# Eight transposes of an attention unit written as one run, and a planner that counts changes of product kind

## The chip, the cores and the metric

The kernel runs on one core of a Trainium2 chip. A core has TensorE (matrix products and transposes, results into PSUM banks), VectorE, ScalarE and GpSimd for everything elementwise, and SyncE (SP), which issues DMAs. In the profile these are PE, DVE, ACT, POOL and SP; PEld is TensorE's loading of the stationary operand. The metric is the device time of one execution in microseconds.

## The reference

Two layers of an encoder trunk on 512 tokens of width 1024, in float32. Cut to what matters:

```
for l in range(DEPTH):                          # DEPTH = 2
    x = x + hybrid_mixer(rms_norm(x), ...)      # 8 heads of neighbourhood attention (NA) beside
                                                # 8 query heads of grouped-query attention (GQA)
    x = x + memory_cross_attention(rms_norm(x), rms_norm(mem), ...)
    x = x + conv_ffn(rms_norm(x), ...)
return rms_norm(x, norm_final)

# both attentions: scores = q k^T (+ bias), p = softmax(scores), o = p v
```

The softmaxed scores p come out with queries on the partitions. For `p v` they are needed with keys on the partitions, so every unit of p is transposed on TensorE.

## The kernel before

Activations lie transposed, channels on partitions and the 512 tokens along the row. A float32 operand is split into a high and a low part of the type fp32r, and a product of two such operands is three matmuls (`mm3`: hi x hi, hi x lo, lo x hi). These are one kind of product. The other kind takes full float32 operands: the transposes (data against `ident`), the sums over partitions (against `ones`) and the rows that spread a norm over the partitions.

Attention is done in units. An NA unit is a pair of heads and two blocks of 128 queries (8 units a layer), a GQA unit a pair of query heads and one block of 128 queries (16 units a layer). Each goes through four steps: scores on TensorE (`na_scores`, `gqa_scores`, into `sc` banks), exponent on ScalarE, division by the sum (`na_normalise`, `gqa_normalise`), transposes (`na_transpose`, `gqa_transpose_p`), values (`na_values`, and `gqa_values` after every fourth unit). `weave` interleaves the steps of successive units, and `Filler` puts the projections, w_out and memory products between them.

A unit has two halves, one per head, each a tile `t` of 128 x 512 scores: four transposes of 128 x 128 into one PSUM bank `tr`, then a cast to the high part on ScalarE and a subtraction for the low part on VectorE (`split_psum`), which frees the bank. There are two `tr` banks. Before, each half asked for its bank, wrote its four transposes and was split, one half after the other. The GQA queries and keys (`gqa_q`, `gqa_k`) are turned in the same manner, four transposes into one bank at a time, through `transposed`.

The order in which TensorE, ScalarE, VectorE and GpSimd do their work is not the written one. `Order`, called at the end, takes every traced instruction, gives it a duration by a table (`Step.times`; a transpose 108 ns, a product of n columns (n + 32) / 2.4 ns), and simulates the engines, the buffers (`SLOTS`) and the DMAs. For TensorE `product_next` looks through up to 240 products not yet issued, in the written order, and takes the first that can start within `PATIENCE` = 60 ns of the engine being free; for the others `choose` goes by due times. It repeats this for 30 rounds with changed due times, replays each with jitter, and keeps the order with the earliest simulated end. SP's queue stays in the written order.

Of the kernel before, what the change touches and what calls it, by code (L numbers as in the profile page):

```python
# [19 lines left out]
P = 128  # L20
# [186 lines left out]
HAND_OVER = {"PE": 60.0, "ACT": 85.0, "DVE": 60.0, "POOL": 80.0, "SP": 60.0}  # L207
STATIONARY = 100.0
FIRST_PRODUCT = 5000.0

# [13 lines left out]
class Step:  # L224
# [5 lines left out]
    def __init__(self, ins, index):  # L230
        self.ins, self.index, self.engine = ins, index, self.ENGINES[ins.engine]
        self.dma = type(ins).__name__ == "InstDMACopy"
        self.reads, self.writes = ([p for p in map(self.part, v) if p] for v in (ins.ins, ins.outs))
        self.names = list(dict.fromkeys(p[0] for p in self.writes + self.reads))
        self.bytes = 4.0 * self.count(ins.outs[0].bass_ap.ap) if self.dma else 0.0
        if self.dma and self.reads:

            self.bytes *= 1.5 if self.writes else 0.4
        self.busy, self.takes = self.times()
        self.sharing = self.shares()  # L240

# [88 lines left out]
class Order:  # L330
# [6 lines left out]

    def __init__(self, tc, kept):
        self.tc = tc
        traced = [i for i in tc.nc.cur_bb.bb.instructions if type(i).__name__ != "BassTilePoolBoundary"]  # L340
# [3 lines left out]
        for s in self.steps:  # L344
            if s.ins.name in kept and s.engine in last:
                self.kept[s.index] = last[s.engine]
            last[s.engine] = s.index
        self.lifetimes()

# [27 lines left out]
    def data(self):  # L377
# [4 lines left out]
        for s in self.steps:  # L382
# [17 lines left out]
            for j in self.before[-1]:  # L400
                self.after[j].append(s.index)

    def wait(self, a, b):
# [49 lines left out]
    def run(self, given=None, draw=None):  # L453
# [16 lines left out]

        moving, clock, last = [], 0.0, 0.0

        def possible(j, ready):

            if need[j] or self.kept.get(j, -1) >= 0 and self.kept[j] not in issued:
                return None
            if j in self.gate and self.gate[j] not in landed:
                return None
            t, wanted = ready[j], {}
            for name in steps[j].names:  # L480
                k = steps[j].kind(name)
                if name not in held and k in slots:

# [109 lines left out]
        while len(issued) < n or moving:  # L593
# [31 lines left out]
            if e == "PE":  # L625
                short = MARGIN - (t - possible(j, fed))
                if product is not None and short > 0:
                    late.append((j, t - product, t - product + short))
                product = t + s.busy
# [26 lines left out]
def encoder_kernel(ctx: ExitStack, tc: tile.TileContext, t: dict, out: bass.AP):  # L656
    nc = tc.nc
    kept = set()
    PE, SP = Counted(nc.tensor), InOrder(tc, nc.sync, kept)
# [496 lines left out]
    for l in range(DEPTH):  # L1156
# [181 lines left out]


        na = {}  # L1340
        parts = [None] * 8
# [40 lines left out]
        def na_transpose(u):  # L1382
            es = na[u]
            pts = []
            for j in range(2):
                tr = ps_t()
                for i in range(2):
                    for c in range(2):
                        PE.transpose(tr[:, (2 * i + c) * P : (2 * i + c + 1) * P], es[j][:, i, c * P : (c + 1) * P], ident)  # L1389
                pt = rtile((2, S))  # L1390
# [64 lines left out]

        def transposed(cc):
            tr = ps_t()
            for c in range(4):
                PE.transpose(tr[:, c * P : (c + 1) * P], cc[:, c * P : (c + 1) * P], ident)  # L1459
            return tr  # L1460

        def gqa_k(xs, cc, sq):
# [11 lines left out]
            def turn():  # L1474
                gk.extend(rtile((2, S)) for _ in range(2))
                split_k(transposed(cc), gk, False)

# [7 lines left out]
        def gqa_q(b, pm):  # L1485
# [11 lines left out]
            def turn():  # L1497
                gq[b] = rtile((2, S))
                split_q(transposed(cc), gq[b])

# [32 lines left out]
        def gqa_transpose_p(u):  # L1533
            es = ga.pop(u)
            i, b = divmod(u, NB)
            if b == 0:
                gpt[i] = []
                for j in range(2):
                    w = xpool.tile([P, KC, S], F32R, tag="xg", name=nm("xg"), bufs=2)
                    gpt[i].append(w.rearrange("p (n k) (b q) -> p n k b q", n=2, q=P))  # L1540
            for j in range(2):
                tr = ps_t()
                for k in range(NB):
                    PE.transpose(tr[:, k * P : (k + 1) * P], es[j][:, k * P : (k + 1) * P], ident)  # L1544
                hi, lo = (gpt[i][j][:, n, :, b] for n in range(2))
# [467 lines left out]

    Order(tc, kept)

# [82 lines left out]
```

## Time and profile before

| | us |
|---|---|
| median of 3 runs | 1315.31 (1315.18 to 1323.04) |
| profiled execution | 1314.66 |
| its span, first to last instruction | 1312.9 |
| TensorE busy in the span | 1302.0 |
| NA units' transposes (L1389), first and last start | 58.7 and 780.0 |
| GQA units' transposes (L1544), first and last start | 144.8 and 865.9 |
| granted TensorE clock | 1.00 |

All times in the traces count from the start of the span. A row of the timeline has the start, the length, the engine, the line, the operation, the tile written and the tiles read, the shape and a count; in brackets stands idle time of the engine before it and what ended it. Matmuls are pipelined: a row's length runs past the start of the next row, so the pace of TensorE is read from start to start. A transpose shows as one matmul of 128 columns.

### The profile page before, as it was taken

How to read it: one execution, taken by the hardware profiler on the slowest of the kernel's cores; microseconds unless marked ns; L12 is line 12 of the kernel's file. 1: busy time of each engine (PE TensorE's matmuls, PEld its weight loads, DVE VectorE, ACT ScalarE, POOL GpSimd, SP SyncE). 2: the span in 40 equal slices, each digit the busy share in tenths (PEclk: the TensorE clock that was granted, in tenths of full speed). 3: DMA queues.
4: the chain of work that ended last, by engine and by line, in shares of the span. 5: the costliest groups of instructions: out<-in, count | busy, mean ns of one | idle time of the engine just before them, and what ended most of it. 6: DMA issues, size and time to landing. Idle time of an engine off the chain costs nothing.

```text
span 1312.9 us, 21053 instructions
## 1 busy us (share of the span) xinstructions
PE 1302.0 (99%) x7632; PEld 1146.1 (87%) x7632; DVE 996.2 (76%) x1858; ACT 786.5 (60%) x1458; POOL 719.9 (55%) x520
## 2 busy tenths in 40 slices
PE   9999999999999999999999999999999999999998
PEld 8888888888789999999888888888887999999987
DVE  6559877675999887788535688776759999877874
ACT  6668876555655555545536688775645555555544
POOL 2757955726454454445746569565454544444443
PEclk9999999999999999999999999999999999999999
DMA  8733322313223333333455523223222333333332
GB/s 255 214 112 112 113 64 66 111 34 113 81 64 105 114 104 100 97 95 103 136 150 169 153 75 108 59 77 91 65 81 85 89 89 105 111 98 89 109 103 76
DMA packets 205000, 136.98 MB, mean 104 GB/s; under 512 B 5600, under 2 KB 195040, under 8 KB 204896
## 3 DMA queue, kind: packets, MB, share of 16 engines
q1 hardware_dynamic: 204080, 134.98, 35.3%
q8 instruction: 60, 0.98, 0.3%
q10 hardware_dynamic: 816, 0.66, 0.2%
q14 instruction: 44, 0.36, 0.1%
HBM read 125.65 MB, written 2.10 MB: 97 GB/s over the span
## 4 chain that ended last, share of the span: by engine, by line
PE 93%; DVE 4%; ACT 2%; issue 1%; DMA 0%; POOLq 0%; POOL 0%; SPq 0%; ACTq 0%; DVEq 0%
PE mm L103 63%; PE sc L103 21%; PE tr L103 4%; PE tr L1544 2%; DVE t L1837 1%; PE tr L1389 1%; PE tr L1731 1%; DVE r L1857 1%; DVE r L1038 0%; ACT hi L742 0%; PE tr L1459 0%; ACT t L1367 0%; DMA xT<-in_xT 0%; DVE xg L1866 0%; DVE t L1447 0%
## 5 line engine op out<-in xcount | busy, mean ns | idle before, releaser
L743 POOL TENSOR_TENSOR lo<-raw,hi 128x512 fp32r<-128x512 f32 (+3 forms) x230 | 369.4, 1620 | 281.0 <-ACT hi L742 233.5
L103 PE MATMUL mm<-r,hi 128*128 128x512 f32 (+1 forms) x1392 | 395.7, 365 | 0.0
L103 PEld LDWEIGHTS mm<-r,hi 128*128 128x128 f32 x1392 | 245.3, 189 | 34.9
L103 PE MATMUL mm<-xg,hi 128*128 128x512 f32 (+1 forms) x960 | 267.7, 364 | 1.5 <-DVE xg L1866 0.6
L103 PE MATMUL mm<-r,lo 128*128 128x512 f32 (+1 forms) x728 | 258.0, 356 | 0.0
L742 ACT CAST hi<-raw 128x512 fp32r<-128x512 f32 (+3 forms) x234 | 167.7, 738 | 134.1 <-PE mm L103 49.9
L103 PEld LDWEIGHTS mm<-xg,hi 128*128 128x128 f32 x960 | 169.9, 189 | 30.8 <-DVE xg L1866 3.3
L103 PE MATMUL mm<-xg,lo 128*128 128x512 f32 (+1 forms) x480 | 173.4, 361 | 0.0
L103 PE MATMUL sc<-r,hi 128*128 128x256 f32 (+1 forms) x832 | 162.9, 291 | 0.0
L754 POOL TENSOR_TENSOR lo<-sf,hi 128x1024 fp32r<-128x1024 f32 x32 | 78.0, 2437 | 148.0 <-ACT hi L751 101.0
L103 PEld LDWEIGHTS mm<-r,lo 128*128 128x128 f32 x728 | 137.5, 189 | 20.0
L103 PEld LDWEIGHTS sc<-r,hi 128*128 128x128 f32 x832 | 133.7, 191 | 4.9
L103 PE MATMUL sc<-r,lo 128*128 128x256 f32 (+1 forms) x416 | 121.2, 291 | 0.0
L751 ACT CAST hi<-sf 128x1024 fp32r<-128x1024 f32 x64 | 67.1, 1048 | 87.6 <-DVE sf L766 38.7
L103 PE MATMUL mm<-hi,xg 128*128 128x512 f32 (+1 forms) x384 | 111.4, 360 | 0.3 <-DVE r L1238 0.3
L103 PEld LDWEIGHTS mm<-xg,lo 128*128 128x128 f32 x480 | 90.7, 189 | 13.9
L754 POOL TENSOR_TENSOR lo<-raw,hi 128x1024 fp32r<-128x1024 f32 x32 | 78.0, 2436 | 43.6 <-ACT hi L751 36.9
L1044 POOL TENSOR_SCALAR t<-t,s 128x512 f32<-128x512 f32 (+1 forms) x112 | 66.8, 611 | 50.0 <-DVE s L1528 27.3
L103 PEld LDWEIGHTS sc<-r,lo 128*128 128x128 f32 x416 | 79.6, 191 | 1.2
L103 PEld LDWEIGHTS mm<-hi,xg 128*128 128x128 f32 x384 | 68.1, 190 | 9.4 <-DVE r L1238 0.6
L103 PE MATMUL sc<-r,r 128*128 128x256 f32 (+1 forms) x352 | 73.9, 330 | 0.0
L103 PE MATMUL mm<-lo,xg 128*128 128x512 f32 (+1 forms) x192 | 68.4, 356 | 0.0
(202 smaller groups left out, 2608.8 us busy)
## 6 DMA issues: line engine op xcount, KB each, us to landing
raw<-in_w_up SPq DMA_DIRECT2D x88, 512.0 KB, 3.8
raw<-in_w_down SPq DMA_DIRECT2D x36, 384.0 KB, 3.5
raw<-in_w_in SPq DMA_DIRECT2D x25, 512.0 KB, 4.8
raw<-in_w_mem_kv SPq DMA_DIRECT2D x16, 512.0 KB, 4.2
raw<-in_w_down SPq DMA_DIRECT2D x24, 320.0 KB, 3.2
r<-in_bias SPq DMA_DIRECT2D x16, 384.0 KB, 5.1
r<-r SPq DMA_DIRECT2D x22, 256.0 KB, 3.5
raw<-in_w_in SPq DMA_DIRECT2D x18, 256.0 KB, 4.7
```

The lines of the kernel that those rows point to most:

```text
L103: return self.engine.matmul(out, lhsT, rhs, **k)
L742: act.copy(hi[:, k], raw[:, k])
L743: (POOL if eng[0] == "P" else DVE).tensor_sub(lo[:, k], raw[:, k], f(hi)[:, k])
L751: act.copy(hi, src)
L754: eng.tensor_sub(lo[:, c], src[:, c], f(hi)[:, c])
L1044: eng.tensor_scalar(e, e, sums[:, col : col + 1], 1.0, op0=ALU.mult, op1=ALU.mult)
L1389: PE.transpose(tr[:, (2 * i + c) * P : (2 * i + c + 1) * P], es[j][:, i, c * P : (c + 1) * P], ident)
L1544: PE.transpose(tr[:, k * P : (k + 1) * P], es[j][:, k * P : (k + 1) * P], ident)
L1731: PE.transpose(tr[:, (2 * c + i) * P : (2 * c + i + 1) * P], e[:, i, c * P : (c + 1) * P], ident)
L1837: DVE.scalar_tensor_tensor(cc[:, dst], u[:, src], wi, cc[:, dst], op0=ALU.mult, op1=ALU.add)
L1857: DVE.scalar_tensor_tensor(xn[c // 2][:, c % 2], xT[c], ffn.gain(c), ffn.psum, op0=ALU.mult, op1=ALU.mult)
```

## The change

A new function `turned` asks for as many `tr` banks as it is given blocks, and writes the four transposes of every block directly after each other. `na_transpose` and `gqa_transpose_p` give it both halves of a unit, so eight transposes; the two splits follow. The queries and keys go through it with one block. The names of the transposes of each call are handed to `Order` as a group.

`Order.together` makes the first transpose of a group wait for everything that any of the group waits for, and has it ask for all the group's banks at once. The planner gets a constant `SWITCH` of 88 ns, which it adds to TensorE's time whenever a product without full float32 operands follows one with them. And after a full-float32 product, `product_next` first looks for another one that can start within 60 ns, before it goes on in the usual way.

```
+SWITCH = 88.0
...
+        self.whole = self.engine == "PE" and any(a.dtype == F32 for a in ins.ins)
...
+    def together(self):
+
+        index, self.banks = {s.ins.name: s.index for s in self.steps}, {}
+        for names in self.groups:
+            mine = [index[n] for n in names]
+            first = mine[0]
+            for j in sorted(set(b for i in mine for b in self.before[i]) - set(mine) - set(self.before[first])):
+                self.before[first].append(j)
+                self.after[j].append(first)
+            self.banks[first] = len({self.steps[i].writes[0][0] for i in mine}) - 1
...
+            if j in self.banks:
+                wanted["tr"] += self.banks[j]
...
         def product_next():
 
             mine, i, seen, best = written["PE"], at["PE"], 0, None
+            if whole:
+                while i < len(mine) and seen < AHEAD_MOST:
+                    j = mine[i]
+                    i += 1
+                    if j in issued:
+                        continue
+                    seen += 1
+                    if steps[j].whole:
+                        t = earliest(j)
+                        if t is not None and max(t, possible(j, fed) + SURE) <= free_at["PE"] + PATIENCE:
+                            return t, j
+                i, seen = at["PE"], 0
...
+            busy = s.busy
+            if e == "PE":
+                busy += SWITCH if whole and not s.whole else 0.0
+                whole = s.whole
...
-            free_at[e] = t + s.busy * slow
+            free_at[e] = t + busy * slow
...
+        def turned(*blocks):
+
+            banks = [ps_t() for _ in blocks]
+            groups.append([
+                PE.transpose(tr[:, c * P : (c + 1) * P], e[:, c * P : (c + 1) * P], ident).ins.name
+                for tr, e in zip(banks, blocks) for c in range(4)])
+            return banks
...
         def na_transpose(u):
-            es = na[u]
             pts = []
-            for j in range(2):
-                tr = ps_t()
-                for i in range(2):
-                    for c in range(2):
-                        PE.transpose(tr[:, (2 * i + c) * P : (2 * i + c + 1) * P], es[j][:, i, c * P : (c + 1) * P], ident)
+            for tr in turned(*(e.rearrange("p i n -> p (i n)") for e in na[u])):
                 pt = rtile((2, S))
                 split_psum(pt[:, 0, :], pt[:, 1, :], tr)
...
-            for j in range(2):
-                tr = ps_t()
-                for k in range(NB):
-                    PE.transpose(tr[:, k * P : (k + 1) * P], es[j][:, k * P : (k + 1) * P], ident)
+            for j, tr in enumerate(turned(*es)):
```

The instructions of every engine are the same in kind and number. Counted in TensorE's order, unbroken stretches of full-float32 products were 127 and are now 93; of them stretches of eight were 17 and are 47, stretches of four 86 and 32. Of TensorE's 7,560 products some 560 stand in another place, in the attention parts most of all, but also in the feed-forward part. SP's queue is unchanged.

Three places. The first is on TensorE, in the NA part of the first layer: the two halves of one unit (tr_1477 and tr_1485, starting at 120.54 and 122.12 us in the trace of before) and tr_1506, a block of GQA queries or keys that takes the bank of tr_1477 next; xg_131 and xg_132 are the high and low part of the normalised input, hi and lo those of a weight. Before:

```order
L1389 MATMUL tr_1477<-ident,t_1305 128x128 x4
L103 MATMUL mm_1390<-hi_1184,xg_131 128x512
L103 MATMUL mm_1390<-lo_1185,xg_131 128x512
L1389 MATMUL tr_1485<-ident,t_1306 128x128 x4
L103 MATMUL mm_1390<-hi_1184,xg_132 128x512
L103 MATMUL mm_1390<-hi_1184,xg_131 128x512
L103 MATMUL mm_1390<-lo_1185,xg_131 128x512
L103 MATMUL mm_1390<-hi_1184,xg_132 128x512
L103 MATMUL mm_1520<-hi_1075,xg_131 128x512
L103 MATMUL mm_1520<-lo_1076,xg_131 128x512
L103 MATMUL mm_1520<-hi_1075,xg_132 128x512
L1459 MATMUL tr_1506<-ident,t_1357 128x128 x4
```

And after, on the same engine from the same transposes on (tr_1478 is what was tr_1485; line 1376 is in `turned`):

```order
L1376 MATMUL tr_1477<-ident,t_1305 128x128 x4
L1376 MATMUL tr_1478<-ident,t_1306 128x128 x4
L103 MATMUL mm_1520<-lo_1076,xg_131 128x512
L103 MATMUL mm_1520<-hi_1075,xg_132 128x512
L103 MATMUL mm_1520<-hi_1075,xg_131 128x512
L103 MATMUL mm_1520<-lo_1076,xg_131 128x512
L103 MATMUL mm_1520<-hi_1075,xg_132 128x512
L103 MATMUL mm_1520<-hi_1089,xg_131 128x512
L103 MATMUL mm_1520<-lo_1090,xg_131 128x512
L1376 MATMUL tr_1506<-ident,t_1357 128x128 x4
```

The two halves are now together and stand behind the products of mm_1390 instead of among them; between the first half's bank and its next use by tr_1506 lie seven products and the second half, where there were nine and the second half.

The second is on TensorE in the GQA part of the first layer, one unit (tr_2050 with its other half) and the scores of a later unit (sc_2067), as one piece of the difference; mm_2093 is a row of the output projection:

```order
-L1544 MATMUL tr_2050<-ident,t_1966 128x128 x4
 L103 MATMUL mm_2093<-r_991,lo_1822 128x512
 L103 MATMUL mm_2093<-r_1273,hi_1821 128x512 x2
 L103 MATMUL mm_2093<-r_1273,lo_1822 128x512
 L103 MATMUL mm_2093<-r_1533,hi_1821 128x512 x2
-L1544 MATMUL tr_2057<-ident,t_1970 128x128 x4
+L103 MATMUL mm_2093<-r_1533,lo_1822 128x512
+L1376 MATMUL tr_2050<-ident,t_1966 128x128 x4
+L1376 MATMUL tr_2051<-ident,t_1970 128x128 x4
 L103 MATMUL sc_2067<-r_1315,r_1713 128x512 x2
```

The first half moved back behind seven projection products to its second half, which itself moved back by one.

The third is on VectorE, which clears the banks, at the next unit of the same part (banks tr_2102 and tr_2109; s_2125 holds the score maxima of a later unit). Before:

```order
L1038 TENSOR_TENSOR xg_2015<-tr_2102,xg_2015 128x4x128
L1519 TENSOR_REDUCE s_2125<-sc_2119 128x1
L1519 TENSOR_REDUCE s_2125<-sc_2120 128x1
L1044 TENSOR_SCALAR s_2125<-s_2125,qr_110 128x1
L1038 TENSOR_TENSOR xg_2016<-tr_2109,xg_2016 128x4x128
```

And after (tr_2103 is what was tr_2109; the lines have moved by 29 to 32):

```order
L1070 TENSOR_TENSOR xg_2015<-tr_2102,xg_2015 128x4x128
L1548 TENSOR_REDUCE s_2125<-sc_2119 128x1
L1548 TENSOR_REDUCE s_2125<-sc_2120 128x1
L1076 TENSOR_SCALAR s_2125<-s_2125,qr_110 128x1
L1070 TENSOR_TENSOR xg_2016<-tr_2103,xg_2016 128x4x128
```

Here nothing moved: although the eight transposes come together, VectorE clears the second bank only behind the maxima of the next scores, as before.

More of the change, by code (lines that the diff above doesn't have):

```diff
@@ L336, with __init__ @@
     ORDERED = FREE + ("PE",)
-    def __init__(self, tc, kept):
-        self.tc = tc
+    def __init__(self, tc, kept, groups):
+        self.tc, self.groups = tc, groups
         traced = [i for i in tc.nc.cur_bb.bb.instructions if type(i).__name__ != "BassTilePoolBoundary"]
@@ L347, in __init__ @@
             last[s.engine] = s.index
+        self.together()
         self.lifetimes()
@@ L469, in run @@
         order, late, product = {e: [] for e in self.ORDERED}, [], None
-        moving, clock, last = [], 0.0, 0.0
+        moving, clock, last, whole = [], 0.0, 0.0, False
         def possible(j, ready):
@@ L628, in run @@
                     late.append((j, t - product, t - product + short))
-                product = t + s.busy
+                product = t + s.busy + (SWITCH if whole and not s.whole else 0.0)
             if s.engine in shared and s.sharing:
@@ L657, in encoder_kernel @@
     nc = tc.nc
-    kept = set()
+    kept, groups = set(), []
     PE, SP = Counted(nc.tensor), InOrder(tc, nc.sync, kept)
@@ L1454, in rotate @@
                 POOL.tensor_add(cc[:, :, a], cc[:, :, a], xs[:, :, b])
-        def transposed(cc):
-            tr = ps_t()
-            for c in range(4):
-                PE.transpose(tr[:, c * P : (c + 1) * P], cc[:, c * P : (c + 1) * P], ident)
-            return tr
         def gqa_k(xs, cc, sq):
@@ L1475, in turn @@
                 gk.extend(rtile((2, S)) for _ in range(2))
-                split_k(transposed(cc), gk, False)
+                split_k(*turned(cc), gk, False)
             late(2, turn)
@@ L1498, in turn @@
                 gq[b] = rtile((2, S))
-                split_q(transposed(cc), gq[b])
+                split_q(*turned(cc), gq[b])
             late(1, norm)
@@ L1540, in gqa_transpose_p @@
                     gpt[i].append(w.rearrange("p (n k) (b q) -> p n k b q", n=2, q=P))
-            for j in range(2):
-                tr = ps_t()
-                for k in range(NB):
-                    PE.transpose(tr[:, k * P : (k + 1) * P], es[j][:, k * P : (k + 1) * P], ident)
+            for j, tr in enumerate(turned(*es)):
                 hi, lo = (gpt[i][j][:, n, :, b] for n in range(2))
@@ L2012, in encoder_kernel @@
             down_last()
-    Order(tc, kept)
+    Order(tc, kept, groups)
 def _head_order():
```

## The prediction

> **What bounds the kernel now.** I read the head of the page first, then the chain of work that ended last, then the list of waits, and then four stretches of the two attention parts.
>
> ```profile
> span 1312.9 us, 21053 instructions
> PE 1302.0 (99%) x7632; PEld 1146.1 (87%) x7632; DVE 996.2 (76%) x1858; ACT 786.5 (60%) x1458; POOL 719.9 (55%) x520
> PE 93%; DVE 4%; ACT 2%; issue 1%; DMA 0%; POOLq 0%; POOL 0%; SPq 0%; ACTq 0%; DVEq 0%
> 60.00:160.00 100.00, 99.08 (x543) 83.80 (x542) 79.55 (x196) 76.05 (x186) 75.78 (x79) 1.00 0.41 122
> 160.00:225.00 65.00, 65.00 (x349) 54.75 (x347) 48.13 (x104) 45.60 (x98) 39.22 (x42) 1.00 0.28 73
> 700.00:800.00 100.00, 99.25 (x538) 83.91 (x537) 75.13 (x188) 73.05 (x179) 67.27 (x72) 1.00 0.42 123
> 800.00:880.00 80.00, 80.00 (x426) 67.30 (x425) 61.97 (x133) 57.56 (x122) 53.40 (x56) 1.00 0.24 67
> PE tr L1389 <- DVE r L1255: 0.8, 2, 0.5
> PE tr L1459 <- DVE r L1038: 0.3, 1, 0.3
> ```
>
> TensorE is busy for 1302.0 of 1312.9 us, and it is 93% of the chain: TensorE bounds the kernel. Its idle time in the whole span is 1312.9 - 1302.0 = 10.9 us. In the stretch rows the columns are the length, then busy time of TensorE, its weight loads, VectorE, ScalarE, GpSimd, then the granted clock. The parts in which the change works, 60 to 225 us and 700 to 880 us, hold 0.92 + 0 + 0.75 + 0 = 1.7 us of idle TensorE. So the rest of the program, which has no attention transposes, could not be helped at all, and the attention parts can be helped by 1.7 us of idle time at most, plus whatever a change of product kind costs inside TensorE. The waits of attention transposes that the profile names are 0.8 + 0.3 = 1.1 us, all on VectorE clearing a bank.
>
> **What a change of kind costs.** This is what the new constant puts at 88 ns, so it is the first term. Two places of the timeline of TensorE:
>
> ```profile
> 183.54 3.34 PE L103 MATMUL mm<-xg,r 128*128 128x512 f32 x14
> 186.73 1.03 PE L1544 MATMUL tr<-ident,t 128*128 128x128 f32 x8
> 187.52 1.17 PE L103 MATMUL sc<-r,r 128*128 128x512 f32 x4
> 188.52 0.62 PE L103 MATMUL mm<-r,hi 128*128 128x512 f32 x2
> ...
> 189.20 0.39 PE L103 MATMUL mm<-r,hi 128*128 128x512 f32 x1
> 189.43 0.60 PE L1544 MATMUL tr<-ident,t 128*128 128x128 f32 x4
> 189.79 0.48 PE L103 MATMUL mm<-r,hi 128*128 128x512 f32 x1
> 190.10 0.40 PE L103 MATMUL mm<-r,lo 128*128 128x512 f32 x1
> ```
>
> The first column is the start. Fourteen 512-column products take 186.73 - 183.54 = 3.19 us, 0.228 each. From the start of a stretch of eight transposes to the product after the next four is 188.52 - 186.73 = 1.79 us; less 4 x 0.228 that is 0.878 for the eight. From the start of a stretch of four to the second product behind it is 190.10 - 189.43 = 0.67; less one product, 0.442. Two stretches of four: 0.884. So joining two stretches saves 0.006 us, with 0.02 us of rounding either way. The product behind a stretch does show 0.48 in place of 0.40 us, and this 0.08 looks like a price of turning. But the last transpose of the stretch hands over early: 189.43 to 189.79 is 0.36 us for four, where half of the stretch of eight is 0.44. What is lost behind is gained ahead, and start to start nearly nothing is left.
>
> TensorE's order has 127 stretches of full-f32 products before and 93 after, 34 fewer. **First term: 34 x 0.006 = 0.2 us saved**, between 0.9 saved and 0.5 lost by the rounding (34 x 0.02 about it). The number of transposes and of other products is the same, and so is SP's queue, row for row.
>
> **The wait of the second half.** In the neighbourhood part a unit is written today as two stretches of four, and one of them waits:
>
> ```profile
> 120.54 0.60 PE L1389 MATMUL tr<-ident,t 128*128 128x128 f32 x4
> 120.90 0.49 PE L103 MATMUL mm<-hi,xg 128*128 128x512 f32 x1
> 121.22 0.39 PE L103 MATMUL mm<-lo,xg 128*128 128x512 f32 x1
> 122.12 0.63 PE L1389 MATMUL tr<-ident,t 128*128 128x128 f32 x4 [0.51 <-DVE r L1255]
> ```
>
> This is the unit of tr_1477 and tr_1485 of the order shown above. Its second half stands 0.51 us for a bank. In the new order the pair stands further back, the second half by five products of 512 columns, 1.1 us, so this wait should go. What is late next is tr_1506, a lone stretch that turns one block of rotated queries or keys and reuses the bank of tr_1477. Before, nine products and a stretch of four lie between the end of the one and the start of the other: 9 x 0.228 + 0.44 = 2.5 us. After, seven: 2.0 us. In the whole new order four such reuses of a bank lie under 2.4 us apart, all at such lone stretches beside neighbourhood units. How long a bank takes to clear is read from the stretch of eight above:
>
> ```profile
> 187.59 1.07 ACT L1037 CAST xg<-tr 128x512 fp32r<-128x512 f32 x2
> 188.20 0.69 DVE L1038 TENSOR_TENSOR xg<-tr,xg 128x512 fp32r<-128x512 f32 x1 [0.70 <-ACT xg L1037]
> 188.81 1.28 DVE L1519 TENSOR_REDUCE s<-sc 128x1 f32<-128x512 f32 x2
> 190.13 0.68 DVE L1038 TENSOR_TENSOR xg<-tr,xg 128x512 fp32r<-128x512 f32 x1
> ```
>
> The stretch ends at 186.73 + 0.88 = 187.61, the second bank is read out at 190.13 + 0.68 = 190.81: 3.2 us, of which 1.28 are score maxima that VectorE takes in between. At worst each of the four reuses waits 3.2 - 2.0 = 1.2 us: 4.8 in all, less the 1.1 that stands there today, 3.7 lost. At best all is hidden and 1.1 is gained. The nearest rows are the waits there today, 0.3 and 0.5 us; I take four of 0.35, so 1.4. **Second term: 1.4 - 1.1 = 0.3 us lost**, between 1.1 gained and 3.7 lost. Queued behind a waiting transpose on TensorE are value products of the unit before and projection products; ScalarE and VectorE have their own backlog meanwhile (76 and 80 of 100 us busy in the first row of stretches), so 0.3 us do not spread.
>
> **The grouped units of the query-block part.** Here a unit's first half moves back by up to 2.5 us of products, and both banks must be empty when it starts. In the new order 16 products of 512 columns lie between most groups: 16 x 0.228 = 3.6 us against 3.2 for clearing, 0.4 us of cover. TensorE idles 0.00 us in 160 to 225 and in 800 to 880 today, with units one after another at about that distance. **Third term: nothing.** If the cover were short by 0.1 us for each of the 32 units, 3.2 us. The value products read the turned scores only after every fourth unit, so moving a unit by 2 us reaches them in one case of four, and there the planner moved them too.
>
> **The plan's clock.** The planner now believes that TensorE spends 0.088 us at each of 93 turns where the rows give 0.006. The order is thus made for a TensorE that is 93 x 0.082 = 7.6 us slower over the whole program than the real one, and it may accept a wait of up to 0.06 us to keep a stretch together. Work of the other engines that the plan has just in time arrives late against the real TensorE. Nothing is lost where they run ahead, which the 0.00 us of idle time in the two query-block stretches show; everything, 7.6 us, where they never do. The bounds are 0 and 7.6, and I take **0.3 us** as the fourth term, nearer to those rows. The same constant rules the search, so rows of the feed-forward part also change places (products of w_down against those of w_up), where nothing changes kind; I cost this at nothing, since no wait of TensorE inside that part is on the list, and VectorE's lead there is what hides it.
>
> **Sum.** -0.2 + 0.3 + 0 + 0.3 = 0.4 us on the profiled execution's own 1314.66 (span 1312.9 and 1.8 around it): 1315.1. That execution lies 0.65 under the median of the runs, 1315.31, so the forecast for a median is **1315.7 us**. Bounds of the terms together: 1.7 of idle time and 0.9 of turns gained, and some 2 us of waits at the borders of the parts, give 1310; 7.6 us of plan lost, and a little of the second term, give 1324.
>
> **The rivals.**
>
> *The turn does cost 88 ns.* For it: the 0.48 against 0.40 us. Against it: the start-to-start sums above. It would give 34 x 0.088 = 3.0 us, so 1315.3 - 3.0 = 1312.3.
>
> *The plan's error shows.* Four or more of the 7.6 us appear as waits: 1319 to 1323. For it: VectorE is near 80% busy in the neighbourhood stretches. Against it: no idle time in the others.
>
> *The pair waits for its slower half (the other side).* Eight transposes now need both halves normalised and both banks empty before the first may start, and TensorE takes its work in order, so the next unit's scores stand behind. If each of the 48 units waited as the one at 122.12 did, 48 x 0.51 = 24.5 us: 1340. It is slower by over 1% from 13.2 / 48 = 0.27 us a unit. For it: the row at 122.12, and cover of only 0.4 us. Against it: 17 units already stand as eights today, such as that at 186.73, with no wait ahead of it.
>
> *A longer stretch of transposes lowers the clock.* TensorE's first products show a slow pace, and the eight of 186.73 a full one:
>
> ```profile
> 1.34 3.27 PE L103 MATMUL tr<-ident 128*128 128x128 f32 x14 [1.34 <-POOL ident masks.py:199]
> 186.50:189.00 2.50, 2.50 (x17) 2.16 (x16) 1.48 (x3) 1.87 (x4) 1.26 (x2) 1.00 0.62 147
> ```
>
> At the start 14 such products take about 3.2 us, 0.23 each, against 0.11 in a stretch of eight. If all eights went at that pace, 47 x 8 x 0.12 = 45 us: 1360. Against it stands the granted clock of 1.00 around an eight. The Trainium skill (TensorE: Matmul & The Clock Gate, Part 4: PE-mode transpose) says that transposes do not count as TensorE being busy for its clock; by that rule, longer stretches of them would be a risk. The trace does not bear it out for 0.88 us of them.
>
> *The change does not group.* The order shows 47 stretches of eight for 48 units, so this is all but excluded; it would give 1315.3.
>
> **How the numbers follow.** The forecast 0.59 (1312.5 to 1319); a turn of 88 ns 0.07; the plan's error 0.19; the pair's wait 0.10; the clock 0.01; no grouping 0.02; a gain of over 1% by something I do not see 0.02. One per cent, 13 us, is about what a measurement of this kernel can tell from no change. A gain of that size is more than all 10.9 us of idle TensorE, hence 0.02. Slower by over 1%: the pair's wait and the clock, 0.11. Within 1%: 0.87. The range 1310 to 1324 holds the forecast, the cheap turn and the plan's error, 0.87 in all.
>
> **What would show it.** In the new profile a stretch of eight should still take 0.88 us, with the product behind it at 0.48 in place of 0.40. TensorE's busy time should be within 1 us of 1302.0, and its idle time 10 to 13 us. The wait of 0.51 at the second half should be gone, and short ones, 0.2 to 0.6 us, stand at lone stretches of four, on VectorE's L1070. The stretches of the query-block part should stay free of idle time. I am wrong if the list of waits has many rows of grouped transposes on VectorE or GpSimd of over 0.27 us each, if the span falls by 3 us with TensorE's busy time, or if the feed-forward part shows idle time that it does not have now.

## The result and the profile after

The changed kernel takes 1322.32 us (median of 11 executions, 1320.96 to 1323.66), the kernel before 1314.93 us on the same chip. The ratio is 1.0049, with a 95% interval of 1.0036 to 1.0063: slower by half a per cent. That is inside the forecast range and within 1%, but it is not the likeliest case of the prediction (1315.7). It is the rival called "the plan's error shows". The kernel before takes 1322.8 to 1324.7 us in 7 of its 96 executions on record, and most ratios here lie lower than the medians would give.

The head of the page of the changed kernel, whose profiled execution took 1323.66 us, and below it the shares of the chain of work that ended last:

```profile
span 1321.9 us, 21038 instructions
PE 1303.7 (99%) x7632; PEld 1146.6 (87%) x7632; DVE 984.3 (74%) x1858; ACT 786.3 (59%) x1458; POOL 725.7 (55%) x520
PE 77%; DVE 10%; ACT 2%; issue 1%; DMA 1%; POOLq 0%; POOL 0%; ACTq 0%; DVEq 0%
```

The span has grown by 9.0 us, TensorE's busy time by 1.7. TensorE idles 1321.9 - 1303.7 = 18.2 us, 7.3 more than before. VectorE's share of the chain has risen from 4% to 10%: there are more places at which TensorE stands for VectorE, although VectorE itself works a little less.

The stretches of the changed kernel, with the columns of the prediction's rows (length, busy time of TensorE, weight loads, VectorE, ScalarE, GpSimd, granted clock, DMA share, GB/s). The third row is the feed-forward part of the first layer, the last the second layer's memory part:

```profile
60.00:160.00 100.00, 97.09 (x529) 81.87 (x529) 77.69 (x191) 75.33 (x183) 74.17 (x81) 1.00 0.40 119
160.00:225.00 65.00, 65.00 (x352) 55.32 (x351) 48.86 (x108) 46.66 (x100) 41.31 (x44) 1.00 0.24 67
330.00:700.00 370.00, 367.65 (x2302) 331.85 (x2302) 286.02 (x462) 196.18 (x299) 188.65 (x98) 1.00 0.36 105
700.00:800.00 100.00, 96.20 (x517) 81.17 (x516) 73.56 (x180) 71.31 (x180) 65.16 (x71) 1.00 0.44 129
800.00:880.00 80.00, 80.00 (x427) 67.38 (x426) 61.04 (x134) 58.81 (x126) 53.67 (x57) 1.00 0.26 73
880.00:985.00 105.00, 104.24 (x512) 87.12 (x511) 66.05 (x137) 60.52 (x109) 56.46 (x32) 1.00 0.27 81
```

Of the kernel before, the two rows of these that the prediction did not show:

```profile
330.00:700.00 370.00, 369.06 (x2311) 333.79 (x2311) 291.57 (x463) 198.34 (x306) 186.00 (x102) 1.00 0.37 108
880.00:985.00 105.00, 104.90 (x513) 87.88 (x511) 68.45 (x142) 61.06 (x110) 57.39 (x31) 1.00 0.29 86
```

Idle TensorE has grown by 99.08 - 97.09 = 2.0 us in the NA part of the first layer, 99.25 - 96.20 = 3.05 in that of the second, 1.4 in the feed-forward part and 0.7 in the second memory part. These are 7.1 of the 7.3 us. The two GQA stretches, where most of the grouped units stand, have none, as before. The granted clock is 1.00 in every stretch shown. TensorE's extra 1.7 us of busy time are no work either: every matmul is the same, and where I count only the places at which the next product starts over 0.1 us behind the pace, there are 46 of 10.2 us in all before and 61 of 19.6 after. The difference, 9.4, covers the span's 9.0.

The list of waits of TensorE in the changed kernel (engine, tile and line that wait; engine, tile and line waited for; us in total, times, the longest):

```profile
PE mm L103 <- DVE xg L1892: 2.5, 5, 1.2
PE tr L1376 <- DVE r L1070: 2.1, 3, 1.5
...
PE tr L1376 <- DVE r L1287: 1.2, 2, 0.7
PE sc L103 <- ACT t L1551: 1.2, 2, 0.7
PE mm L103 <- DVE r L1070: 1.1, 1, 1.1
```

L1376 is the transpose in `turned`. Its waits, 2.1 + 1.2 us in five places, are all for a bank: each of the five starts 0.15 us after VectorE has read a bank out. L1070 reads the banks of units, L1287 those of query blocks. The 2.1 us stand at three lone stretches of four, each a query block that needs the bank of a unit (0.26, 0.30 and 1.50 us). The 1.2 us stand inside two grouped eights of the NA parts, 0.69 and 0.54 us, between the fourth and the fifth transpose: the first half of the unit is done, and the bank of the second still holds a query block. The first of the two, on TensorE and then on VectorE:

```profile
129.85 0.60 PE L1376 MATMUL tr<-ident,t 128*128 128x128 f32 x4
131.15 0.63 PE L1376 MATMUL tr<-ident,t 128*128 128x128 f32 x4 [0.69 <-DVE r L1287]
```

```profile
129.61 1.39 DVE L1287 TENSOR_TENSOR r<-tr,r 64x512 fp32r<-64x512 f32 x2
```

The plan gives a group both banks at once. On the chip the first half begins as soon as its own bank is free. The first row of the list is at the entrance of the feed-forward parts: L1892 makes the low part of their normalised input.

The longest wait of a transpose, in the NA part of the second layer; first on TensorE, then on VectorE:

```profile
757.97 1.03 PE L1376 MATMUL tr<-ident,t 128*128 128x128 f32 x8
758.76 0.48 PE L103 MATMUL mm<-hi,xg 128*128 128x512 f32 x1
...
760.21 0.51 PE L103 MATMUL sc<-r,r 128*128 128x256 f32 x3
762.23 0.63 PE L1376 MATMUL tr<-ident,t 128*128 128x128 f32 x4 [1.50 <-DVE r L1070]
```

```profile
757.48 1.73 DVE L1119 SCALAR_TENSOR_TENSOR r<-r,par,r 128x256 fp32r<-128x256 f32 x1 [1.12 <-ACT r L1118]
...
759.69 0.59 DVE L1119 SCALAR_TENSOR_TENSOR r<-r,par,r 128x256 fp32r<-128x256 f32 x1
760.21 1.28 DVE L1482 TENSOR_TENSOR t<-mm,r 128x512 f32<-128x512 f32 x2
761.41 1.27 DVE L1070 TENSOR_TENSOR r<-tr,r 128x512 fp32r<-128x512 f32 x2
```

The eight ends at 757.97 + 0.88 = 758.85. VectorE reads its banks only at 761.41, because its order puts two L1119 and two rotations (L1482), among others, in front. The first L1119 takes 1.73 us, where the shortest of its line takes 0.48; GpSimd works beside it, and it ends 0.28 us after an instruction of GpSimd's (758.93). TensorE reaches the lone stretch, which needs one of these banks, after nine products, three of them of 256 columns, and stands. So the run of eight is not slow: the read-out comes late against the TensorE that is really there, by VectorE's order and by the long L1119. How much each is worth here is not separated.

The entrance of the feed-forward part of the first layer, one row each of VectorE, GpSimd and TensorE:

```profile
344.65 2.23 DVE L1892 TENSOR_TENSOR xg<-r,xg 128x512 fp32r<-128x512 f32 x1
```

```profile
343.35 5.79 POOL L775 TENSOR_TENSOR lo<-raw,hi 128x1024 fp32r<-128x1024 f32 x2 [10.26 <-ACT hi L774]
```

```profile
346.94 0.50 PE L103 MATMUL mm<-xg,hi 128*128 128x512 f32 x1 [1.20 <-DVE xg L1892]
```

The median of the 16 L1892 instructions is 0.68 us. This one takes 2.23 while GpSimd splits a weight, and TensorE waits 1.20 us for it. The order puts the weight's split just there.

### The profile page after: what moved, and what is told of

The parts are those of the page before. It is cut to its first block, busy times and chain, and to the rows that moved or that the text cites. A ratio compares the mean times of both kernels' runs of the same rounds, so it can differ in the third digit from the quotient of the medians.

```text
span 1321.9 us, 21038 instructions
## 1 busy us (share of the span) xinstructions
PE 1303.7 (99%) x7632; PEld 1146.6 (87%) x7632; DVE 984.3 (74%) x1858; ACT 786.3 (59%) x1458; POOL 725.7 (55%) x520
## 4 chain that ended last, share of the span: by engine, by line
PE 77%; DVE 10%; ACT 2%; issue 1%; DMA 1%; POOLq 0%; POOL 0%; ACTq 0%; DVEq 0%
PE mm L103 50%; PE sc L103 20%; PE tr L103 4%; PE tr L1376 2%; DVE t L1863 2%; DVE xg L1892 1%; DVE r L1070 1%; DVE r L1883 1%; ACT hi L774 1%; PE tr L1757 1%; DVE r L1287 1%; DMA r<-r 1%; DVE t L1482 0%; DVE r L1905 0%; DVE r L1119 0%
## 5 line engine op out<-in xcount | busy, mean ns | idle before, releaser
L786 POOL TENSOR_TENSOR lo<-raw,hi 128x1024 fp32r<-128x1024 f32 x32 | 82.6, 2581 | 42.7 <-ACT hi L783 41.1
L1076 POOL TENSOR_SCALAR t<-t,s 128x512 f32<-128x512 f32 (+1 forms) x112 | 66.5, 608 | 64.2 <-DVE s L1557 37.6
L1070 DVE TENSOR_TENSOR r<-tr,r 128x512 fp32r<-128x512 f32 x80 | 54.1, 686 | 21.6 <-ACT r L1069 17.7
```

The costliest lines, as they stand in the source:

```text
L786: eng.tensor_sub(lo[:, c], src[:, c], f(hi)[:, c])
L1070: DVE.tensor_sub(lo, ps, f(hi))
L1076: eng.tensor_scalar(e, e, sums[:, col : col + 1], 1.0, op0=ALU.mult, op1=ALU.mult)
```

## The experiments

The expectations call the theories by letters. P: the price of 88 ns in the plan is at fault. G: the grouping itself is. S: it is the luck of the search, which would give another time for any change of its numbers. T and D came up later, when P did not hold in its simple form. T: what matters is that the price stands at the turns. D: what matters is that the simulated run has time in it that the due times do not have. All are compared with the kernel before on the same chip:

| run | us | before | ratio (95%) |
|---|---|---|---|
| the change | 1322.32 | 1314.93 | 1.0049 (1.0036 to 1.0063) |
| e1: price 0 | 1315.83 | 1315.55 | 0.9994 (0.9975 to 1.0012) |
| e2: halves apart, price 88 | 1320.46 | 1315.55 | 1.0024 (1.0008 to 1.0040) |
| e3: grouping alone | 1314.66 | 1315.55 | 0.9982 (0.9966 to 0.9998) |
| e4: the change, other seed | 1324.90 | 1315.55 | 1.0063 (1.0045 to 1.0082) |
| e5: before, other seed | 1316.57 | 1315.02 | 1.0012 (1.0002 to 1.0021) |
| e10: price 6 | 1315.41 | 1315.02 | 1.0003 (0.9993 to 1.0012) |
| e11: price 88, no preference | 1319.46 | 1315.02 | 1.0033 (1.0020 to 1.0046) |
| e12: before, transposes 22 ns dearer | 1317.09 | 1315.02 | 1.0010 (0.9997 to 1.0023) |
| e13: grouping alone, other seed | 1314.80 | 1315.07 | 0.9990 (0.9974 to 1.0005) |
| e15: price 44 | 1314.67 | 1315.07 | 0.9989 (0.9973 to 1.0004) |
| e16: grouping alone, run 7.8 us slower | 1318.60 | 1315.07 | 1.0019 (1.0004 to 1.0034) |
| e17: price 88 in the due times too | 1324.25 | 1315.07 | 1.0044 (1.0018 to 1.0070) |

Differences given in us below are those of the medians in this table.

### The change taken apart: e1, e2, e3

Grouping and preference, without the price:

```
-SWITCH = 88.0
+SWITCH = 0.0
```

> The change with the price of a turn at 0 instead of 88 ns; the units stay grouped and a full-f32 product still draws the next one. Before is 1314.9 us, the change 1322.3. Theory P (the 7.6 us that the plan counts for turns and the chip does not take make work late): 1315 to 1317, with idle TensorE back near 11 us. Theory G (the grouping itself: both halves and both banks needed at once): stays at 1321 to 1324. Theory S (any new order of the search lands some us off, by luck): anywhere from 1314 to 1324, with the waits in other places than in the change.

Measured 1315.83, 0.3 us above the kernel before. The loss is gone with one number of the plan.

Price and preference, without grouping. Each half goes through `turned` by itself:

```
-            for tr in turned(*(e.rearrange("p i n -> p (i n)") for e in na[u])):
+            for e in na[u]:
+                tr, = turned(e.rearrange("p i n -> p (i n)"))
...
-            for j, tr in enumerate(turned(*es)):
+            for j in range(2):
+                tr, = turned(es[j])
```

> The change with the two halves of every unit written and grouped apart again, four transposes and one bank at a time; the price of 88 ns and the preference for the next full-f32 product stay. P: 1320 to 1324, since the plan's clock is as wrong as in the change (with more turns, rather more). G: back to 1314 to 1316. S: anywhere from 1314 to 1324.

Measured 1320.46, 4.9 us above. The first rows of its waits look like those of the change:

```profile
PE tr L1376 <- DVE r L1287: 3.0, 3, 1.1
PE mm L103 <- DVE xg L1894: 1.7, 2, 1.1
```

Here no unit is grouped by force, and still TensorE waits for bank read-outs and at the entrance of the feed-forward part (L1894 is L1892 of the change). The grouping is not needed for the loss.

Grouping alone, neither price nor preference:

```
-SWITCH = 88.0
+SWITCH = 0.0
...
-            if whole:
+            if False:
```

> The units grouped in eights, but the planner as before: no price of a turn and no preference. P: 1314 to 1317. G: 1321 to 1324. S: anywhere from 1314 to 1324; and if G and S are both wrong, this one has eight transposes in one stretch with TensorE's idle time at 11 us as before the change.

Measured 1314.66, with a ratio of 0.9982 whose interval ends just under 1; by the medians it is 0.07% faster than before. The waits of its transposes for units and blocks:

```profile
PE tr L1376 <- DVE r L1287: 1.1, 2, 0.8
PE tr L1376 <- DVE s L1076: 0.8, 2, 0.4
PE tr L1376 <- POOL t L1076: 0.4, 1, 0.4
```

L1076 is a helper that scales: the division by the sum on GpSimd, the score maxima on VectorE. The names in the last two rows mislead. One of these places, the second half of a grouped GQA unit, on TensorE and then on VectorE:

```profile
211.72 0.63 PE L1376 MATMUL tr<-ident,t 128*128 128x128 f32 x4 [0.41 <-DVE s L1076]
```

```profile
210.88 0.68 DVE L1070 TENSOR_TENSOR xg<-tr,xg 128x512 fp32r<-128x512 f32 x1
211.48 0.21 DVE L1076 TENSOR_SCALAR s<-s,qr 128x1 f32<-128x1 f32 x1
```

GpSimd's division had ended at 209.37. The transposes start 0.16 us after the read-out of a bank (210.88 + 0.68 = 211.56), as at the waits of the change; the small L1076 only lies in between. So this is a wait for the second bank, and so is every row of the list: the two on L1287 and the two on VectorE's L1076 are at second halves of four grouped units, 2.0 us in all, the last at a lone stretch. That is a part of the rival "the pair waits", at four units of 48, and this kernel is as fast as the one before all the same. Theory G falls.

### The luck of the search: e4, e5, e13

The planner's search starts from a number that only seeds its random jitter:

```
-ROUNDS, REPLAYS, MARGIN, SHARES, STRETCH, SEED = 30, 4, 100.0, (0.0, 0.0, 0.5, 1.0, 2.0), 500, 4
+ROUNDS, REPLAYS, MARGIN, SHARES, STRETCH, SEED = 30, 4, 100.0, (0.0, 0.0, 0.5, 1.0, 2.0), 500, 5
```

In the changed kernel:

> The change unaltered but for the start value of the planner's random draws (5 for 4), so another order under the same rules. P and G: 1320 to 1325, as the change, with waits at lone stretches of transposes in the neighbourhood parts. S: differs from 1322.3 by more than 2 us one way or the other, with the waits elsewhere.

In the kernel before:

> The kernel before with another start value of the planner's random draws (5 for 4) and nothing else. P: within 2 us of 1315, since the plan's clock is right. S (luck of the search alone): differs from 1315 by as much as the change does, 5 us or more.

In the kernel with grouping alone (e3):

> Units grouped, planner as before the change, other start value of the random draws. With the start value of the change this kernel took 1314.66 us, 0.18% under before. If grouping by itself is worth something: 1315 or less again, under the 1316.6 of the kernel before with this start value. If that was the luck of one order: 1315 to 1318.

Measured 1324.90, 1316.57 and 1314.80. Each taken against its kernel before, another seed moves the change by 2.0 us (9.4 against 7.4), the kernel before by 1.6 and grouping alone by 0.6 (-0.3 against -0.9). With either seed the changed kernel stands 7 us or more above the kernel before of the same seed (7.4 and 1324.90 - 1316.57 = 8.3). S explains the scatter and not the loss. The changed kernel with the other seed has more waits at the feed-forward entrance:

```profile
PE mm L103 <- DVE xg L1892: 4.4, 6, 1.3
```

### Is the loss proportional to the price: e10, e15, e11

The price that the trace of before supports:

```
-SWITCH = 88.0
+SWITCH = 6.0
```

> The change with the price of a turn at the 6 ns that the start-to-start sums give, all else as in the change. P: 1314 to 1317. If any counting of turns did harm, or the preference did: 1319 or more.

Measured 1315.41. Its two NA stretches, and then its first waits:

```profile
60.00:160.00 100.00, 97.19 (x530) 81.99 (x529) 79.90 (x192) 75.09 (x183) 73.50 (x78) 1.00 0.40 118
700.00:800.00 100.00, 99.70 (x538) 84.62 (x537) 77.18 (x190) 73.92 (x183) 67.62 (x72) 1.00 0.40 122
```

```profile
PE mm L103 <- DVE r L1270: 1.6, 1, 1.6
...
PE tr L1376 <- DVE s L1076: 0.7, 2, 0.4
PE tr L1376 <- DVE r L1287: 0.6, 1, 0.6
```

In the second layer the 3.8 us of idle TensorE of the change are 0.3. In the first it is as much as in the change, with 1.6 us of it in one wait that is no transpose. The waits of transposes for banks, those named L1076 with them, are 1.9 us in all, against 3.3 in the change.

Half the price:

```
-SWITCH = 88.0
+SWITCH = 44.0
```

> The change with half the price of a turn, 44 ns. The plan then counts about 92 x 0.038 = 3.5 us that the chip does not take, against 7.5 us at 88 ns. P, if every microsecond counted too much is paid back as waiting: 1317.5 to 1320, half way between 1315.4 (price 6) and 1322.3 (price 88). If the loss has a threshold: at one of the two ends.

Measured 1314.67: no loss at all, where P in its simple form, a loss in proportion to the time wrongly counted, asked for half. Its NA stretches are at least as full as those of the kernel before in the second layer (TensorE busy for 99.75 of 100 us, 99.25 before), and about as full in the first (98.99, 99.08 before).

By the 0.006 us of the prediction the plan counts 92 x 0.038 = 3.5 us too many here and loses nothing; at 7.6 us it loses 7. The loss is no straight line between the two.

The price without the preference for another full-float32 product:

```
-            if whole:
+            if False:
```

> The change without the preference for a next full-f32 product; units grouped, price 88 ns. P: 1320 to 1324, the price alone is enough. If it took the preference together with the price: 1314 to 1317.

Measured 1319.46, 4.4 us above the kernel before and just under the 1320 that P asked for. With the preference it is 7.4. Without a price the preference makes 1.2 us of difference (e1 against e3, 1315.83 and 1314.66). These are single orders, and another seed moves one by up to 2.0 us. So all four kernels with a price of 88 ns in the simulated run alone (e2, e4, e11 and the change) lose, 4.4 to 9.4 us, and what the preference adds is not settled. The number of turns is 90 to 94 in every grouped kernel, with a price or without: the price buys no fewer turns.

Which waits go with the loss? Not those for banks. They are 1.2 us before and 3.3 in the change, but 3.0 with a price of 0 (e1), 2.3 in e3, 1.9 in e10 and 0.4 in e15, and only 1.8 in e11 and 2.2 in e4, which lose. The waits at the feed-forward entrance do go with it. They are 0.6 us before, 0.7, 0.3, 0.3 and 0.8 in e1, e3, e10 and e15, which lose next to nothing, and 1.7, 2.4, 2.5 and 4.4 in e2, e11, the change and e4, and 1.7 in e16 below. They are only a part of the loss: 1.9 of the 7.3 us by which the idle time of the change has grown.

### Which kind of wrong clock: e12, e16, e17

The kernel before, with a wrong duration of another place. Its 488 transposes in the plan get 22 ns too much, 10.7 us in all, in due times and in the run alike:

```
-                return 108.0, 280.0
+                return 130.0, 302.0
```

> The kernel before with no grouping and no price of a turn, but with the planner's duration of a transpose at 130 ns instead of 108 (its latency lengthened alike): the same kind of error, put in elsewhere. 488 transposes x 22 ns = 10.7 us that the plan counts and the chip does not take. P: slower than before by 4 to 11 us, 1319 to 1326, with TensorE idle in the neighbourhood parts. G and S, and a theory in which only turns matter: 1314 to 1317.

Measured 1317.09, 2.1 us above by the medians, with an interval of the ratio that still holds 1. P asked for more, so P in its simple form misses here too: not every slow clock of this size costs 7 us.

The kernel with grouping alone, with 16 ns more for each transpose, 7.8 us in all, in the simulated run only:

```
-            busy = s.busy
+            busy = s.busy + (16.0 if e == "PE" and s.ins.is_transpose else 0.0)
```

> Units grouped, no price of a turn, no preference (the kernel of 1314.7), but in the simulated run of the plan every transpose keeps TensorE 16 ns longer, 488 x 16 = 7.8 us in all, while the due times are worked out from the true durations, as in the change. P (any time counted too much on TensorE in the simulated run): 1319 to 1323. D (it is the split that counts: a simulated clock later than the due times): the same, 1319 to 1323, where the earlier run with 130 ns in both gave 1317.1. Theory T (only a price at the turn itself does harm, since it sits where the next product's operands are handed over): 1314 to 1317.

Measured 1318.60, 3.5 us above the kernel before, where the same kernel without it (e3) was 0.9 below its own, and a little under the 1319 that P and D asked for. No price stands at the turns here, so the loss does not need T. Its longest wait, 1.9 us, stands inside the feed-forward part, at 380.76. The next is at the entrance again:

```profile
PE mm L103 <- DVE xg L1892: 1.7, 3, 0.8
```

The changed kernel with its price in the due times as well:

```
-        start, now = {}, FIRST_PRODUCT
+        start, now, whole = {}, FIRST_PRODUCT, False
...
+                now += SWITCH if whole and not s.whole else 0.0
+                whole = s.whole
```

> The change with the 88 ns counted in the due times as well, turn by turn in the written order. P: stays at 1320 to 1324, the simulated clock is as wrong as before. D: falls to 1315 to 1318. T: stays at 1320 to 1324.

This kernel has two levels, and its median can't be read without them: 3 of 10 executions took 1314.43, 1315.09 and 1316.26, the other 7 took 1323.63 to 1324.74. The profiled one is of the upper level, 1324.43. Its list of waits has one row that the others have not:

```profile
PE mm L103 <- DVE t L1452: 7.8, 1, 7.8
```

VectorE and GpSimd at that place:

```profile
781.47 8.96 DVE L1121 SCALAR_TENSOR_TENSOR r<-r,par,r 128x256 fp32r<-128x256 f32 x1
```

```profile
781.34 5.01 POOL L777 TENSOR_TENSOR lo<-raw,hi 128x512 fp32r<-128x512 f32 x4
786.28 1.42 POOL L1491 TENSOR_TENSOR t<-t,t 128x256 f32<-128x256 f32 x2
787.64 2.50 POOL L777 TENSOR_TENSOR lo<-raw,hi 128x512 fp32r<-128x512 f32 x2
```

One L1121 takes 8.96 us, and L1452, for which TensorE waits, comes behind it at 790.91. The shortest of its line takes 0.47 (466 ns in the group's row):

```profile
L1121 DVE SCALAR_TENSOR_TENSOR r<-r,par,r x16: 466/632/8956, 102.8 to 796.2; 128x256 fp32r<-128x256 f32 x16
```

It starts 0.13 us after the start of a run of GpSimd without a break, 781.34 to 790.14, and ends 0.29 us after that run does. TensorE loses 7.8 us there, and then some more: the granted clock is down to half.

```profile
786.00:796.00 10.00, 4.53 (x11) 3.60 (x12) 9.81 (x16) 3.11 (x8) 4.14 (x5) 0.50 0.46 139
```

From 791.47, where TensorE goes on, to 795.88 ten products of 512 columns take 4.41 us, where ten take 2.28 at the usual pace: 2.1 us more. Together that is about the distance between the levels, some 9 us. Without that meeting the kernel would probably be at the level of the three: as fast as the kernel before, though its price is 88. That is what D asks for. The kernel before has long executions of 1322.8 to 1324.7 us as well, if fewer, so such a level is not peculiar to this order; what happens in them is not shown. And seven executions of ten are hidden behind one accident, I have no profile of the lower level, and three executions are few. So D fits the results (run alone slower: e16, e11, e2, e4 and the change lose 3.5 to 9.4; both slower: e12 loses 2.1, e17 at its lower level next to nothing), except e15, where the run alone counts 4.0 us and nothing is lost. D is suggested and not shown.

One more number speaks against a simple story of collisions. I added up, over all VectorE instructions of each profiled execution, the time above the lower quartile of their kind (line, tiles and shape), where that is over 0.15 us. It is 67 us before, 68 in e1, 71 in e3, and higher where the run alone counts extra time: 80 in e2, 82 in e11, 85 in the change, 90 in e16. But it is 83 in e15 and 75 in e10 too, which lose nothing or next to nothing.

## Why the prediction was right and wrong

- **What bounds the kernel.** Right: 7.3 of the 9.0 us of the span are idle TensorE. The argument from idle time, though, only limits what can be gained; it sets no limit to what a worse order can lose. The recorded 1322.32 us lies inside the range by the upper bound of the fourth term, not by the forecast, and with some luck: the same change with another seed (e4) takes 1324.90, above the range.
- **First term, what a turn costs.** Right in kind and a little small. An eight in the GQA part of the changed kernel:

```profile
189.15 1.03 PE L1376 MATMUL tr<-ident,t 128*128 128x128 f32 x8
189.94 1.17 PE L103 MATMUL sc<-r,r 128*128 128x512 f32 x4
190.94 0.39 PE L103 MATMUL mm<-r,hi 128*128 128x512 f32 x1
```

  From 189.15 to 190.94 are 1.79 us, less 4 x 0.228: 0.878, as before. The prediction's 0.006 us for a turn is the difference of two rounded sums. Over the clean stretches of the trace of before (512-column products around them, no wait), the time from the product ahead to the third product behind has a median of 1.135 us for 30 stretches of four and 1.569 for 20 of eight. Two of four against one of eight and three products more (0.681): 0.02 us a turn, so 0.7 us for the 34, inside the bounds. By this the plan counts some 0.07 us too many at each turn, 6.3 us for 93, in place of 7.6, and about 2.2 in place of 3.5 at a price of 44. The rival of a turn of 88 ns, which would have saved 3 us, falls.
- **Second term, banks at lone stretches.** Right in part. Lone stretches do wait on VectorE's L1070 in the NA parts, three of them, 2.1 us. But the wait of the second half did not go: it is gone at the unit of 122.12 and stands at the second halves of two other units, 0.69 and 0.54 us, where 0.51 and 0.31 stood before. So I set 1.4 us, and the rows give 2.1 + 1.2 = 3.3. Less the 1.1 of before, 2.2 in place of 0.3, within the bounds. The price is not what makes the difference: with a price of 0 these waits are 3.0 us, with 6 ns 1.9. The term itself was too small.
- **Third term, grouped GQA units.** Right for the change: 0.00 us of idle time in the two GQA stretches. Where the price is small the cover is short at some grouped units: in e3 two of them in these stretches wait 0.4 us each for the second bank, behind the maxima of the next scores.
- **Fourth term, the plan's clock. This is the step that failed.** I set 0.3 us "nearer to those rows", the two GQA stretches without idle time. Against their kernels before, the change (7.4) and the price of 6 (0.4) lie 7.0 us apart by their medians, 6 by their ratios: 6 to 7 in place of 0.3. The bounds of 0 and 7.6 held. The rows were true and stayed true, but they were the wrong place: those stretches have cover, and a slow clock shows where there is none, in the NA parts (5.0 us, though 2.0 of them, in the first layer, stand at a price of 6 too) and at the entrances of the parts behind. "The feed-forward part at nothing" was wrong for the same reason: its inside is covered, its entrance is not (1.4 us more in that stretch, with one wait of 1.20 at 346.94). New idle time there was one of the signs of error that I had named.
- **The sizes for "what would show it".** TensorE's busy time is 1.7 us up where I asked for at most 1, the idle time 18.2 where I asked for 10 to 13.
- **The rivals.** The pair's wait of 0.27 us or more at each unit does not occur: it stands at two of the 48 units of the change, 1.2 us in all, and for a bank, not for a half not yet normalised. The clock is 1.00 in every stretch shown. The grouping is there.
- **The chances.** The plan's error had 0.19 by the reasoning "for it VectorE's 80%, against it the GQA rows". The first should have weighed more. The three cases named for the range add up to 0.85; the 0.87 has the 0.02 of "no grouping" in it.

What stays open: how the price makes its waits, why 44 ns cost nothing and 88 ns 7 us, and whether the due times without the price are what does the harm. The orders are the outcome of a search of 30 rounds, one order for each kernel, so the time need not follow the price smoothly.

## What to carry to other kernels

A planner's duration has to be the start-to-start distance in a trace. The product behind a turn is drawn 0.08 us longer, but start to start it costs 0.006 to 0.02 more, and a price near the drawn difference made the order worse by some 7 us while the edit that it came with was worth 0 to 2. Look for the cost of a wrong duration where TensorE waits already, not in the stretches that have none. Judge such an edit in parts: grouping alone gave 1314.66 and 1314.80 us (0.2% better than before at the most), and the same grouping with the price 1322 to 1325.

## What the runs showed of the hardware

A VectorE instruction that reads two operands from SBUF can be held while GpSimd works. In the change an L1892 takes 2.23 us in place of 0.68. It ends 0.55 us after the GpSimd instruction that it met (346.33), while GpSimd's next one is already running. That is the usual case: in the 14 profiled executions 944 VectorE instructions take over 0.5 us more than the shortest of their kind, and 924 of them last until behind the end of one GpSimd instruction, 19 of two, and one of eight. This last is the 8.96 us in place of 0.47 in e17, held for the whole of an unbroken run of GpSimd. I had not reckoned with a hold of that length, and why VectorE got no turn between the eight is not shown. The Trainium skill (GPSIMD Engine Reference, 1. Specifications) says that GpSimd shares its interfaces to SBUF with VectorE, so that the two contend when a VectorE instruction has two SBUF inputs, as both of these have; the trace agrees, and adds how long it can last.

The long wait of e17 had a second price, the clock. TensorE stood from 783.68, the granted clock fell to 0.5 at 785.9 and came back at 796.1, 4.6 us after TensorE went on. A 512-column product took 0.43 us from start to start in between, in place of 0.23.
